# A gate group's silus queued behind a head's casts, and attention begun two filler steps sooner, in a hybrid attention and recurrence layer

## The chip, the core and the metric

The kernel runs on one core of a Trainium2 chip. TensorE (PE; PEld are its weight loads), VectorE (DVE), ScalarE (ACT) and GpSimd (POOL) each have an instruction queue of their own, and so has SyncE (SP), which here only issues transfers. The metric is the device time of one execution in microseconds, and the profile is of one execution taken by the hardware profiler.

## The reference

One layer on a residual stream x of 512 tokens by 2048 features: an RMSNorm, one input projection, an attention group beside a gated recurrence, a gate on each, and one output projection.

```python
h = rms_norm(x, norm_w)
proj = jnp.einsum('bsd,de->bse', h, w_in)                 # 2048 -> 4608
q, k, v, g_attn, xr, g_lru = jnp.split(proj, SPLITS, axis=-1)
attn_out = attention_group(q, k, v, q_norm_w, k_norm_w)   # 8 heads of 128, 2 key heads
lru_out = lru_group(xr, conv_w, conv_b, ...)              # two scans, added
mixed = jnp.concatenate([rms_norm(attn_out, attn_norm_w) * jax.nn.silu(g_attn),
                         rms_norm(lru_out, lru_norm_w) * jax.nn.silu(g_lru)], axis=-1)
return x + jnp.einsum('bse,ed->bsd', mixed, w_out)
```

In the attention group q and k get an RMSNorm and a rotary embedding per head, then softmax(q k / sqrt(128)) v over all 512 tokens. All is float32.

## The kernel before

Every operand of a matmul is split into a high and a low part of a shorter format, and `mm3` (L151) forms a product from three matmuls, high by high, high by low and low by high. A weight chunk is 256 rows by 512 columns: loaded into the ring `wr` (L205, on SP), cast by ScalarE to `wh` (L216) and subtracted by VectorE to `wl` (L217).

The stages are: the projection of the recurrence's input, with the recurrences woven into the next projections; keys and values; two query groups; then the stage that the change touches; the last gate projection; and the output projection (L901) with pre-added weights. Those pre-added weights are made by transfers between DRAM blocks, which run during the earlier stages: `last_sums` (L792) hands out one for each score step of the attention, first eight accumulating transfers on POOL (L777), then eight copies on SP (L774), then sixteen accumulating ones.

The stage in question weaves two generators on TensorE, in an order written out by hand (`manual_schedule` for PE, and for SP too):

- `gates` (L1129) is the filler: the projections of three gate groups of 512 columns, 32 filler steps each. A filler step is six matmuls into one of four PSUM banks `pj`; four steps use up one weight chunk, and eight chunks fill the four banks of a group. With the 33rd step the group's four banks are evacuated (`evac_bc`, L390, VectorE, raised to the highest priority) and `gate` (L676) emits the group's four silus at once, on the evacuated tiles `ev` in place (L682, ScalarE). Four products with the recurrence's output `hs` follow, one at every fourth filler step (L686). The first two groups do so inside this stage; the third's gate comes later, with `sig` given.
- `attention` (L649) is the chain. `turned` (L580) transposes a head's queries on TensorE (L548) and splits them: ScalarE casts the high part (L552), VectorE subtracts the low one (L553). Score step i stands for head h = i // 4 and token block t = i % 4. `weights` (L588) does its scores (three matmuls), their maximum `mx` on VectorE (L598), the exp on ScalarE (L600), the reciprocal of the sum (L601), the scaling on POOL (L602) and a 32 by 32 block transposition on VectorE into `u` (L603). At t = 0 of the next head `moved` (L608) writes `u` aside to DRAM (`pd`, L611), and at t = 2 it reads it back turned (`pt`, four transfers, L616) and splits it into `ph` by two casts on ScalarE (L624) and `pl` by two subtractions on VectorE (L625); `pt`, `ph` and `pl` have one buffer each. `values` (L629) multiplies `ph` and `pl` with the values, at score step 4h + 10 for head h: 12 matmuls. `first` in `weights` queues the maximum and exp of step 4h + 9 behind the casts and subtractions of head h.

`weave` takes BEGIN filler steps first and STEPS behind each score step; BEGIN is 12 (three chunks), STEPS 2.

TensorE and SP follow the program's order here. The order on ScalarE, VectorE and POOL is set when the kernel is built, by a planner that simulates the program with costs of its own and issues, among what is ready, what has the higher priority; `high_priority(n)` raises a block as if it stood n instructions earlier (AHEAD is 600, used for weight loads too), and `issue_after(ins)` queues what a block puts on `ins`'s engine behind `ins`. On the chip each engine keeps to that order.

Of the kernel before, what the change touches and what calls it, by code (L numbers as in the profile page):

```python
# [13 lines left out]
AF = mybir.ActivationFunctionType  # L14
# [22 lines left out]
AHEAD = 600  # L37
# [5 lines left out]
WARM, WARM2 = 14, 5  # L43


BEGIN, STEPS, LATE = 12, 2, 3


H = 256
# [13 lines left out]
def hybrid_kernel(  # L63
# [20 lines left out]
    nc = tc.nc  # L84
# [45 lines left out]
    def at(tag, bufs, shape, dt=F32):  # L130
        return pools["att"].tile([P, *shape], dt, tag=tag, bufs=bufs, name=nm(tag))
# [60 lines left out]
    def v1(r):  # L192
        return vec[:, r : r + 1]
# [350 lines left out]
    def turn(rot, h):  # L544

        pt = mm()
        for t in range(NT):
            nc.tensor.transpose(pt[:, t * P : (t + 1) * P], rot[t][:, h, :], ident)  # L548
        return pt

    def split_ps(pt, hi, lo):
        nc.scalar.copy(hi, pt)  # L552
        nc.vector.tensor_sub(lo, pt, f(hi))  # L553
# [26 lines left out]
    def turned(rot, h):  # L580

        q = at("q", 2, (2, SEQ), F32R)
        split_ps(turn(rot, h), q[:, 0, :], q[:, 1, :])
        return q[:, 0, :], q[:, 1, :]

    last_scale = [None]

    def weights(q, g, t, turned_, first=()):  # L588

        qh, ql = q  # L590
        tt = slice(t * P, (t + 1) * P)
        sc = mm()
        mm3(sc, qh[:, tt], ql[:, tt], kth[g], ktl[g], True, True)
        mx, sm = (at(n, 6, (1,)) for n in ("mx", "sm"))
        with ExitStack() as stack:
            for ins in first:
                stack.enter_context(tc.issue_after(ins))
            nc.vector.tensor_reduce(mx, sc, axis=AX.X, op=ALU.max, negate=True)  # L598
            p = at("p", 3, (SEQ,))
            nc.scalar.activation(p, sc, AF.Exp, bias=mx, accum_out=sm)  # L600
        nc.vector.reciprocal(sm, sm)  # L601
        last_scale[0] = nc.gpsimd.tensor_scalar(p, p, sm, 0.0, op0=ALU.mult, op1=ALU.add).ins  # L602
        nc.vector.transpose(  # L603
            turned_[:, :, :, t, :].rearrange("p a s c -> p s a c"),
            p.rearrange("p (s a c) -> p s a c", a=NQ, c=B),
        )

    def moved(turned_):  # L608

        aside_ = dram.tile([P, NQ, NT * P], F32, name=nm("pd"), tag="pd", bufs=NH)  # L610
        nc.sync.dma_start(aside_, turned_.rearrange("p a s t c -> p a (s t c)"))  # L611
        yield
        pt = at("pt", 1, (NQ, NT, P))
        src = aside_.rearrange("(i r) a x -> a r i x", r=B)
        for a in range(NQ):
            nc.sync.dma_start(  # L616
                pt[a * B : (a + 1) * B].rearrange("p i s x -> p i (s x)"), src[a]
            )
        hi, lo = at("ph", 1, (NT, SEQ), F32R), at("pl", 1, (NT, SEQ), F32R)
        hi4, lo4 = (v.rearrange("p s (i x) -> p i s x", i=NQ) for v in (hi, lo))  # L620
        for s in range(0, NT, 2):
            ss = slice(s, s + 2)
            last = [
                nc.scalar.copy(hi4[:, :, ss], pt[:, :, ss]).ins,  # L624
                nc.vector.tensor_sub(lo4[:, :, ss], pt[:, :, ss], f(hi4[:, :, ss])).ins,  # L625
            ]
        yield hi, lo, last

    def values(h, hi, lo):  # L629

        gs = slice(h // G * HD, (h // G + 1) * HD)
        o = mm()
        for s in range(NT):
            mm3(o, vh[s][:, gs], vl[s][:, gs], hi[:, s], lo[:, s], s == 0, s == NT - 1)
        if h % 2 == 0:
            ap_[h // 2] = aring.tile([P, 2, SEQ], F32, name=nm("av"))
        av, asum = ap_[h // 2][:, h % 2, :], sums["a"]
        nc.vector.tensor_copy(
            av.rearrange("p (t i c) -> p i t c", i=NQ, c=B),
            o.rearrange("p (i t c) -> p i t c", i=NQ, c=B),  # L640
        )
        if h == 0:
            nc.scalar.activation(asum, av, AF.Square)
        else:
            sq = at("p", 3, (SEQ,))
            nc.scalar.activation(sq, av, AF.Square)
            nc.gpsimd.tensor_add(asum, asum, sq)

    def attention(rots, transfers):  # L649

        qs, pts = {h: turned(rots[0], h) for h in range(1)}, {}
        yield BEGIN
        last = NH * NT
        for i in range(last + NT + LATE):
            h, t = divmod(i, NT)
            if i < last:
                if t == 0:
                    u = at("u", 2, (NQ, NT, NT, B))
                first = pts[h - 2][2] if h > 1 and t == 1 else ()
                weights(qs[h], h // G, t, u, first)  # L660
                next(transfers, None)
                if t == 0 and h + 1 < NH:
                    qs[h + 1] = turned(rots[(h + 1) // G], (h + 1) % G)
                if t == NT - 1:
                    pts[h] = moved(u)
            if t == 0 and 0 < h <= NH:
                next(pts[h - 1])
            if t == 2 and 0 < h <= NH:
                pts[h - 1] = next(pts[h - 1])
            h, t = divmod(i - LATE, NT)  # L670
            if t == NT - 1 and h > 0:
                values(h - 1, *pts.pop(h - 1)[:2])
            yield STEPS + (last <= i < last + NT)


    def gate(gs, pairs, row, sig):  # L676

        for e, g in enumerate(gs):
            if e == 0 or sig:
                ss = [sig()] if sig else gs  # L680
                for s, src in zip(ss, [g] if sig else gs):
                    nc.scalar.activation(s, src, AF.Silu)  # L682
            s = ss[0] if sig else g
            yield 4
            dst = pairs[e // 2][:, e % 2, :]
            nc.vector.scalar_tensor_tensor(dst, dst, v1(row + e), s, op0=ALU.mult, op1=ALU.mult)  # L686
# [409 lines left out]
    rots = []  # L1096
# [32 lines left out]
    def gates():  # L1129
        todo = iter(())  # L1130
        for n, (c0, row) in enumerate(((C_GL, R_LN), (C_GL + SEQ, R_LN + 4), (C_GA, R_AN))):
            acc, wait = [], 0
            for k, _ in enumerate(proj_feat(c0, acc, take=take)):
                if n == 0 and k >= 16 and k % 4 == 0:
                    normed(hp[k // 4 - 4])
                if wait == 0:
                    wait = next(todo, 99)
                wait -= 1
                yield
            if n < 2:  # L1140
                todo = gate(evac_bc(acc), hp[2 * n : 2 * n + 2], row, None)
            else:
                late.extend(evac_bc(acc))
# [4 lines left out]
    with tc.manual_schedule(engines={mybir.EngineType.SP}):  # L1148
        weave(fill, attention(rots, last_sums()))
# [23 lines left out]
    def later():  # L1173
        yield 2
        with tc.high_priority():
            r = group_rstd(sums["a"], "r_a", NH * HD)
        yield 4
        with tc.high_priority():
            rows(gbc, r, lambda: fin_s((P, NT, P), F32R))
        for pair in ap_[:2]:  # L1180
            normed(pair)
        yield 4
        todo = gate(late, ap_[:2], R_AN, fin_s)
        for _ in range(3):
            yield next(todo)
        build(4, ap_[0], [hring.tile([P, 7, H], F32R, name=nm(t)) for t in ("mh", "ml")])
        yield from todo
        for pair in ap_[2:]:
            normed(pair)
# [15 lines left out]
    def last_gates():  # L1205
        gs = evac_bc(acc)
        yield
        drain(gate(gs, ap_[2:], R_AN + 4, fin_s))
        yield
        yield  # L1210
        build(5, ap_[1], kept("out", 5))
        yield
        yield
        build(6, ap_[2], kept("out", 6))
        yield
        build(7, ap_[3], kept("out", 7))
        yield
# [49 lines left out]
```

## Time and profile before

| | us |
|---|---|
| time, median of 3 runs (lowest, highest) | 651.07 (650.69, 651.70) |
| the profiled execution: its time | 651.64 |
| its span, first to last instruction | 649.9 |
| TensorE busy | 636.7 |
| VectorE busy | 490.3 |
| ScalarE busy | 339.9 |
| the stage with the attention, first to last score matmul | 272.4 to about 411 |

A row of the timeline gives start and length in us, the engine, the line of the kernel, the operation, the tile written and those read, the shapes, the number of instructions in one row and, in brackets, how long the engine stood idle before it and what ended that. A row of several instructions has the time from the first's start to the last's end. A matmul's length is longer than the distance to the next one's start, since matmuls overlap: distances of starts tell the pace. A row of waits names the engine that waited, the tile and line, what it waited for, and the total, number and longest of those waits.

### The profile page before, as it was taken

How to read it: one execution, taken by the hardware profiler on the slowest of the kernel's cores; microseconds unless marked ns; L12 is line 12 of the kernel's file. 1: busy time of each engine (PE TensorE's matmuls, PEld its weight loads, DVE VectorE, ACT ScalarE, POOL GpSimd, SP SyncE). 2: the span in 40 equal slices, each digit the busy share in tenths (PEclk: the TensorE clock that was granted, in tenths of full speed). 3: DMA queues.
4: the chain of work that ended last, by engine and by line, in shares of the span. 5: the costliest groups of instructions: out<-in, count | busy, mean ns of one | idle time of the engine just before them, and what ended most of it. 6: DMA issues, size and time to landing. Idle time of an engine off the chain costs nothing.

```text
span 649.9 us, 8237 instructions
## 1 busy us (share of the span) xinstructions
PE 636.7 (98%) x2835; PEld 522.9 (80%) x2835; DVE 490.3 (75%) x788; ACT 339.9 (52%) x582; POOL 102.4 (16%) x137
## 2 busy tenths in 40 slices
PE   9999999999999999999899979999999999999996
PEld 7888888888888888888688758888888888888885
DVE  5889689977688963855877786547987867787775
ACT  3533899489856615434643464435545544434441
POOL 0000100112013301243123414301000001020010
PEclk9999999999999999999999989999999999999999
DMA  9844685857467331359889789982336676797152
GB/s 293 290 136 124 143 208 150 198 152 163 127 194 264 99 97 33 98 96 262 273 233 220 195 219 213 237 243 76 97 102 222 187 267 206 270 357 235 65 196 97
DMA packets 62074, 119.23 MB, mean 183 GB/s; under 512 B 5336, under 2 KB 15696, under 8 KB 61008
## 3 DMA queue, kind: packets, MB, share of 16 engines
q1 hardware_dynamic: 54000, 100.87, 49.1%
q0 software_dynamic: 7712, 17.31, 14.5%
q10 hardware_dynamic: 320, 0.53, 0.3%
q8 instruction: 22, 0.36, 0.2%
q14 instruction: 20, 0.16, 0.1%
HBM read 106.10 MB, written 33.55 MB: 215 GB/s over the span
## 4 chain that ended last, share of the span: by engine, by line
PE 81%; issue 6%; POOL 4%; DVE 3%; DMA 3%; ACT 2%; DVEq 0%; POOLq 0%; ACTq 0%
PE pj L152 16%; PE pj L153 16%; PE pj L154 16%; PE mm L901 11%; PE pj L901 9%; PE mm L153 3%; PE mm L154 3%; PE mm L152 3%; POOL p L602 2%; POOL t L777 1%; PE mm L242 1%; DMA wr<-in_x_dram 1%; DMA pd<-u 1%; PE pj L308 1%; DMA pt<-pd 1%
## 5 line engine op out<-in xcount | busy, mean ns | idle before, releaser
L152 PE MATMUL pj<-x,wh 128*128 128x512 f32 x376 | 148.2, 394 | 0.0
L154 PE MATMUL pj<-x,wl 128*128 128x512 f32 x376 | 146.9, 391 | 0.0
L153 PE MATMUL pj<-x,wh 128*128 128x512 f32 x376 | 146.8, 391 | 0.0
L216 ACT CAST wh<-wr 128x512 fp32r<-128x512 f32 x143 | 84.2, 618 | 88.1 <-PE pj L154 26.0
L217 DVE TENSOR_TENSOR wl<-wr,wh 128x512 fp32r<-128x512 f32 x144 | 101.7, 742 | 29.1 <-ACT wh L216 29.0
L753 ACT CAST wh<-wr 128x1024 fp32r<-128x1024 f32 (+1 forms) x72 | 60.6, 860 | 75.1 <-PE mm L901 35.3
L754 DVE TENSOR_TENSOR wl<-wr,wh 128x1024 fp32r<-128x1024 f32 (+1 forms) x72 | 68.6, 985 | 25.0 <-ACT wh L753 24.9
L154 PEld LDWEIGHTS pj<-x,wl 128*128 128x128 f32 x376 | 70.7, 188 | 15.2
L152 PEld LDWEIGHTS pj<-x,wh 128*128 128x128 f32 x376 | 70.8, 188 | 14.7
L153 PEld LDWEIGHTS pj<-x,wh 128*128 128x128 f32 x376 | 70.8, 188 | 14.6
L152 PE MATMUL pj<-wh,x 128*128 128x512 f32 x192 | 74.9, 390 | 0.0
L154 PE MATMUL pj<-wh,x 128*128 128x512 f32 x192 | 74.7, 389 | 0.0
L153 PE MATMUL pj<-wl,x 128*128 128x512 f32 x192 | 74.7, 389 | 0.0
L777 POOL DMA_DIRECT2D t<-in_w_out_dram x40 | 34.4, 867 | 101.6 <-DMA t<-in_w_out_dram 101.1
L901 PE MATMUL mm<-wh,mh 128*128 128x512 f32 x128 | 49.8, 389 | 0.0
L901 PE MATMUL mm<-wl,mh 128*128 128x512 f32 x128 | 49.8, 389 | 0.0
L901 PE MATMUL mm<-wh,ml 128*128 128x512 f32 x128 | 49.8, 389 | 0.0
L600 ACT ACTIVATE p<-mm,mx 128x512 f32<-128x512 f32 x32 | 22.0, 688 | 51.6 <-DVE mx L598 51.4
L154 PEld LDWEIGHTS pj<-wh,x 128*128 128x128 f32 x192 | 36.0, 188 | 7.6
L152 PEld LDWEIGHTS pj<-wh,x 128*128 128x128 f32 x192 | 36.1, 188 | 7.4
L153 PEld LDWEIGHTS pj<-wl,x 128*128 128x128 f32 x192 | 36.1, 188 | 7.4
L602 POOL TENSOR_SCALAR p<-p,sm 128x512 f32<-128x512 f32 x32 | 24.7, 772 | 103.6 <-DVE sm L601 97.7
(204 smaller groups left out, 1062.0 us busy)
## 6 DMA issues: line engine op xcount, KB each, us to landing
wr<-in_w_in_dram SPq DMA_DIRECT2D x71, 512.0 KB, 4.1
wr<-in_w_out_dram SPq DMA_DIRECT2D x24, 512.0 KB, 5.1
t<-in_w_out_dram POOLq DMA_DIRECT2D x40, 256.0 KB, 6.1
wr<-t SPq DMA_DIRECT2D x40, 256.0 KB, 4.7
pd<-u SPq DMA_DIRECT2D x8, 1024.0 KB, 6.6
pt<-pd SPq DMA_DIRECT2D x32, 256.0 KB, 6.1
t<-in_w_out_dram SPq DMA_DIRECT2D x24, 256.0 KB, 5.8
t<-t SPq DMA_DIRECT2D x16, 256.0 KB, 7.3
```

The costliest lines, as they stand in the source:

```text
L152: nc.tensor.matmul(acc, lh, rh, start=start, stop=False)
L153: nc.tensor.matmul(acc, lh, rl, start=False, stop=False)
L154: nc.tensor.matmul(acc, ll, rh, start=False, stop=stop)
L216: copy(hi, raw[:, k, :])
L217: nc.vector.tensor_sub(lo, raw[:, k, :], f(hi))
L242: nc.tensor.transpose(pt[:, t * P : (t + 1) * P], xc[:, t, ks], ident)
L600: nc.scalar.activation(p, sc, AF.Exp, bias=mx, accum_out=sm)
L602: last_scale[0] = nc.gpsimd.tensor_scalar(p, p, sm, 0.0, op0=ALU.mult, op1=ALU.add).ins
L753: nc.scalar.copy(hi[:, to], b)
L754: nc.vector.tensor_sub(lo[:, to], b, f(hi[:, to]))
L777: nc.gpsimd.dma_start(dst, src, accum_op=ALU.add)
L901: nc.tensor.matmul(dst[s], lh[:, ts_], rh, start=i == 0 and j == 0, stop=i == 7 and j == 2)
```

## The change

Three edits. BEGIN goes from 12 to 10 filler steps. The first head's queries are turned and split inside `high_priority(AHEAD)`. And `pts`, the table of heads whose probabilities are under way, becomes visible to `gate`, which queues its silus behind the second high-part cast of every head in it that has its parts (an entry that is a tuple; `parts[2][0]` is that cast on ScalarE).

```diff
-BEGIN, STEPS, LATE = 12, 2, 3
+BEGIN, STEPS, LATE = 10, 2, 3
...
     last_scale = [None]
+    pts = {}
...
     def attention(rots, transfers):
 
-        qs, pts = {h: turned(rots[0], h) for h in range(1)}, {}
+        with tc.high_priority(AHEAD):
+            qs = {0: turned(rots[0], 0)}
         yield BEGIN
...
         for e, g in enumerate(gs):
             if e == 0 or sig:
                 ss = [sig()] if sig else gs
-                for s, src in zip(ss, [g] if sig else gs):
-                    nc.scalar.activation(s, src, AF.Silu)
+                with ExitStack() as stack:
+                    for parts in pts.values():
+                        if isinstance(parts, tuple):
+                            stack.enter_context(tc.issue_after(parts[2][0]))
+                    for s, src in zip(ss, [g] if sig else gs):
+                        nc.scalar.activation(s, src, AF.Silu)
```

When the gates with `sig` run, after the attention, `pts` is empty and nothing is queued behind anything.

## The prediction

> **What bounds the kernel now.** The page's first row comes first: TensorE is busy in all but 2% of the span. So time can only come out of the places where it stands still or slows down, and the view of waits on TensorE names them.
>
> ```profile
> PE 636.7 (98%) x2835; PEld 522.9 (80%) x2835; DVE 490.3 (75%) x788; ACT 339.9 (52%) x582; POOL 102.4 (16%) x137
> ...
> PE mm L152 <- ACT ph L624: 3.9, 2, 3.4
> PE mm L153 <- DVE pl L625: 2.9, 3, 1.5
> ```
>
> Both large waits are for the split probabilities `ph` and `pl` of a head, in `values`. The stretches of 10 us show where (columns: start and end, length, busy PE, PEld, DVE, ACT, POOL, granted clock, DMA share, GB/s):
>
> ```profile
> 310.00:320.00 10.00, 7.78 (x33) 5.89 (x33) 9.89 (x16) 7.00 (x13) 1.36 (x2) 1.00 0.80 234
> ...
> 380.00:390.00 10.00, 5.93 (x17) 4.12 (x16) 9.21 (x13) 6.86 (x11) 0.56 (x1) 0.75 0.87 247
> 390.00:400.00 10.00, 10.00 (x41) 8.12 (x40) 5.48 (x12) 3.58 (x10) 6.61 (x7) 0.91 0.93 163
> ```
>
> In the second place the granted clock falls too, to 0.75 and 0.91 in these stretches. TensorE's timeline at both places, with an undisturbed head (346 us) between them as the measure:
>
> ```profile
> 308.77 0.40 PE L154 MATMUL mm<-kt,q 128*128 128x512 f32 x1
> 309.72 0.50 PE L152 MATMUL mm<-ph,v 128*128 128x512 f32 x1 [0.55 <-ACT ph L624]
> 311.77 0.50 PE L153 MATMUL mm<-pl,v 128*128 128x512 f32 x1 [1.55 <-DVE pl L625]
> ...
> 314.11 0.50 PE L153 MATMUL mm<-pl,v 128*128 128x512 f32 x1 [0.67 <-DVE pl L625]
> ...
> 315.38 0.39 PE L152 MATMUL pj<-x,wh 128*128 128x512 f32 x1
> ...
> 346.48 0.39 PE L154 MATMUL mm<-kt,q 128*128 128x512 f32 x1
> 349.28 0.39 PE L154 MATMUL mm<-ph,v 128*128 128x512 f32 x1
> ...
> 380.92 0.40 PE L154 MATMUL mm<-kt,q 128*128 128x512 f32 x1
> 384.69 0.56 PE L152 MATMUL mm<-ph,v 128*128 128x512 f32 x1 [3.37 <-ACT ph L624]
> 385.95 0.80 PE L153 MATMUL mm<-pl,v 128*128 128x512 f32 x1 [0.70 <-DVE pl L625]
> ...
> 391.97 0.39 PE L152 MATMUL pj<-x,wh 128*128 128x512 f32 x1
> ```
>
> From a head's last score matmul to its last value matmul are 12 starts; undisturbed they take 349.28 - 346.48 = 2.80 us, 0.233 each. The first filler matmul behind is start 13, so 3.03 us. At the first place it comes 315.38 - 308.77 = 6.61 us later: **3.58 us lost**. At the second, 391.97 is start 16 (three filler matmuls, 0.23 each, are in between), due after 3.72 us, but comes after 11.05: **7.33 us lost**, 4.07 of it the marked waits and most of the rest 14 starts at 0.43 us (385.95 to 391.97) instead of 0.23. Together 10.9 us.
>
> Why `ph` is late is on ScalarE:
>
> ```profile
> 305.77 1.28 ACT L682 ACT_TABLE_LOAD   x1
> 307.06 0.63 ACT L682 ACTIVATE ev<-ev 128x512 f32<-128x512 f32 x1
> ...
> 308.63 1.98 ACT L624 CAST ph<-pt 128x1024 fp32r<-128x1024 f32 x2
> ...
> 311.56 1.15 ACT L682 ACTIVATE ev<-ev 128x512 f32<-128x512 f32 x2
> 314.73 1.28 ACT L600 ACT_TABLE_LOAD   x1 [2.03 <-DVE mx L598]
> ...
> 377.71 1.28 ACT L682 ACT_TABLE_LOAD   x1
> ...
> 381.81 0.63 ACT L682 ACTIVATE ev<-ev 128x512 f32<-128x512 f32 x1 [1.55 <-DVE ev L390]
> ...
> 383.61 1.98 ACT L624 CAST ph<-pt 128x1024 fp32r<-128x1024 f32 x2
> ```
>
> A gate group's silus (L682) and their table load stand ahead of the `ph` casts: two silus at 307, four from 379 on, where ScalarE also waits for an evacuation (L390). That the data was not what was late, the chain of waits says:
>
> ```profile
> 294.61 4.99 DMA pt<-pd
> ```
>
> The transposed probabilities of head 0 had landed by 299.6, 9 us before their casts began.
>
> **The change, part by part.** I count score steps i (four to a head, `weights`) and filler steps (six matmuls, 12 x 6 starts from 255.95 to 272.41 below, 1.372 us each).
>
> *Silus behind the high parts.* The gate group is emitted with filler step 33. Before, that followed score step 10 = 12 + 2 x 10; now it follows 11, and likewise 27 in place of 26. `pts` then holds head 1 (or 5) as a tuple, so the silus queue behind that head's second `ph` cast. There is one `ph` buffer, so this cast in turn comes after head 0's values: all silus leave the place ahead of `ph` 0 and `ph` 4. Nothing is added: the same 8 silus, the same table loads. Removed from the path: up to 3.58 + 7.33 us.
>
> What then sets `ph` is the planner's usual order, `ph` behind the exp of step 4h+8. Heads 3 and 5 show its margin:
>
> ```profile
> 362.96 2.32 DVE L625 TENSOR_TENSOR pl<-pt,ph 128x1024 fp32r<-128x1024 f32 x2
> 364.20 0.19 PEld L153 LDWEIGHTS mm<-pl,v 128*128 128x128 f32 x1 [0.46 <-DVE pl L625]
> ...
> 401.62 2.31 DVE L625 TENSOR_TENSOR pl<-pt,ph 128x1024 fp32r<-128x1024 f32 x2
> 405.08 0.40 PE L152 MATMUL mm<-ph,v 128*128 128x512 f32 x1
> ```
>
> Head 5's first `pl` half ends about 402.8, and the second value matmul wants it at 405.3: 2.5 us to spare. Head 3 had -0.46, by the weight load's wait. The gate heads carry in addition the evacuations L390 on VectorE, which are raised above everything:
>
> ```profile
> 309.89 0.69 DVE L390 TENSOR_TENSOR ev<-pj,rbc 128x512 f32<-128x512 f32 x1
> ```
>
> With the values now before filler steps 31 and 32, two of the four banks can be evacuated ahead of them: 2 x 0.69 = 1.4 us in front of `pl`. By head 5's margin that costs 0, by head 3's 0.46 + 1.4 = 1.9 us. I take 0.4 a gate, nearer to head 5, since the gate products (L686), which need the silus, leave this place on VectorE with them: **0.8 us left of the 10.9**, bounds 0 and 3.8.
>
> *Where the silus go.* Behind head 1's casts ScalarE has a gap now:
>
> ```profile
> 324.28 1.99 ACT L624 CAST ph<-pt 128x1024 fp32r<-128x1024 f32 x2
> ...
> 330.25 0.69 ACT L600 ACTIVATE p<-mm,mx 128x512 f32<-128x512 f32 x1 [2.94 <-DVE mx L598]
> ```
>
> The block is 1.28 + 2 x 1.15 + 1.28 = 4.9 us; 2.9 hide in the gap, so the exps of steps 13 and 14 come some 2 us late. The next thing this could hold is head 2's `ph` behind exp 16, with head 5's 2.5 us margin: I cost it at nothing. Without the gap it would be 4.9 - 2.5 = 2.4 us a gate. Queued behind the silus are the four gate products (L686), now some 12 us later; their result is read only after the attention.
>
> On the price of the switch the Trainium skill speaks against the change: "ScalarE: Activation LUTs", section "What ACT_TABLE_LOAD costs", puts about 1.38 us of drain on top of the 1.28 us load. Here the load at 305.77 ends at 307.05 and the silu starts at 307.06, so no row shows the drain; with it the block would be 7.6 us by an estimate from that page, and about 2.2 us a gate would be lost.
>
> *First scores two filler steps sooner* (BEGIN 10). All attention work moves 2.74 us ahead of the projection: scores, exps, `pd` and `pt` transfers on SP, one accumulating DMA (L777) on POOL per step. On SP the `pd` and `pt` issues stay ahead of the same weight loads; a 256 KB `t<-t` copy moves in front of some, which ring and fetch-ahead cover. By itself this gains nothing: TensorE runs the same matmuls. What it needs is query 0:
>
> ```profile
> 255.95 0.48 PE L152 MATMUL pj<-x,wh 128*128 128x512 f32 x1
> ...
> 268.40 0.59 ACT L552 CAST q<-mm 128x512 fp32r<-128x512 f32 x1 [0.84 <-DVE ev L536]
> ...
> 269.02 1.29 DVE L217 TENSOR_TENSOR wl<-wr,wh 128x512 fp32r<-128x512 f32 x2
> 270.22 0.68 DVE L553 TENSOR_TENSOR q<-mm,q 128x512 fp32r<-128x512 f32 x1
> ...
> 272.41 0.40 PE L152 MATMUL mm<-kt,q 128*128 128x512 f32 x1
> ```
>
> The scores move to 255.95 + 10 x 1.372 = 269.67; the third matmul of `mm3`, 0.47 us later at 270.14, wants the low part, which now ends at 270.90. *Queries at higher priority*: the cast at 268.40 waits for a rope product on VectorE, so it can't go much sooner; but the subtraction can pass the two L217 and end near 269.7. So the wait is 0 (it passes) to 0.76 us (it doesn't); I take **0.2**. If ScalarE stands at this cast, two weight casts stand behind it, with one chunk (four filler steps) of cover; without it 1.1 us.
>
> *Sum.* The profiled execution is 651.64 us (span 649.9 and 1.74 around it). 651.64 - 10.9 + 0.8 + 0.2 = 641.7. It lies 0.57 above the median of 651.07, so **641.2 us** against the median; own range 639.8 (all 10.9 and head 3's 0.46 saved) to 644.8 (all bounds: 3.0 and 0.56 more).
>
> The clock term rests on rows: 4.07 us of waits brought 0.75 and 0.91, while 2.77 us at the first place left 1.00. The Trainium skill, "TensorE: Matmul & The Clock Gate", Part 1, gives the array a half-rate clock after an idle window of about 3.4 us and one busy window to recover. The trace agrees with the 0.43 us starts; by it, too, a remaining wait of 1 to 2 us costs no clock.
>
> **The rivals.** *The silu block is cut up.* If the planner sets exps between the silus, they need another pair of table loads, 2.56 us: exps 1.9 + 2.6 = 4.5 us late, less the 2.5 us margin 2.0 us on heads 2 and 6, together 4.0: **645.2**. For it: the evacuations come in one by one, and silus with them (two, a pause, two, above). Against: behind `ph` 1 all four evacuations are done.
>
> *A switch holds ScalarE for longer than its load.* If each of the block's two switches took a second load's length, 1.28 us, the block would be 7.4 us, the exps again 4.5 late: **645.2**. Against it the silu starts 0.01 us behind its load. This is the drain of the page named above.
>
> *The gain is given back elsewhere:* the `ph` casts stay late for another reason on the two engines, so that only the silus' place changes: **651**. Against it is the landing at 299.6.
>
> *Slower.* The half-chunk shift puts weight splits in front of `pl`. Filler chunks now end before odd score steps, in the middle of each head's cast and split:
>
> ```profile
> 351.93 4.12 DVE L217 TENSOR_TENSOR wl<-wr,wh 128x512 fp32r<-128x512 f32 x2
> ...
> 353.00 1.89 POOL L647 TENSOR_TENSOR asum<-asum,p 128x512 f32<-128x512 f32 x1
> ```
>
> A pair took 4.12 us here instead of 1.29, beside POOL work. If such a pair lands before `pl` in every head, 4.12 - 2.5 = 1.6 us is lost eight times, 13 us, on top of the 641.2: **654**. It decides from 9.9 / 8 = 1.24 us a head on, where nothing of the gain is left. Against: the chunk's buffers come free only at score step 4h+9, when the casts behind exp 4h+8 have usually begun, and the other pair of each head moves away from the values' POOL work.
>
> **How the numbers follow.** Forecast (641.2) 0.66; cut-up silus 0.10 and longer switches 0.04 (645.2); given back (651) 0.05; slower (654) 0.15. About 0.2%, here 1.3 us, is what a measurement of this kernel can tell from no change: faster is below 649.8, 0.66 + 0.10 + 0.04 = 0.80; same 0.05; slower 0.15. The range leaves out the last two cases and starts with the forecast's own: 639.8 to 649.8.
>
> **What would show it.** Right: L682 only behind the `ph` casts of heads 1 and 5; the waits for `ph` and `pl` on TensorE down from 6.8 us to under 2; granted clock 1.00 from 300 to 400; first score matmul near 269.7. Wrong: new TensorE waits at heads 2 and 6 (cut-up silus, or longer switches), in every head's `values` with L217 ahead of L625 (slower), or at the first score for `q`.

## The result and the profile after

| | before | after |
|---|---|---|
| time, median (lowest, highest), us, 20 runs each on the same chip | 651.57 (649.77, 652.95) | 650.84 (647.40, 653.39) |
| span of the profiled execution, us | 649.9 | 649.9 |
| ratio to before, 95% interval | | 0.9991 [0.9978, 1.0005] |

No change that this measurement can tell, where 641.2 us were forecast. (New lines of the kernel stand up to six later: the exp is L601, `pd` L612, `pt` L617, `ph` L625, `pl` L626, the silus L688, the accumulating transfers L783.) The waits of TensorE in the changed kernel:

```profile
PE pj L152 <- ACT wh L216: 3.3, 1, 3.3
PE mm L153 <- DVE pl L626: 3.0, 3, 1.7
...
PE pj L154 <- DVE wl L217: 0.8, 1, 0.8
PE mm L154 <- DVE q L553: 0.6, 1, 0.6
```

The waits for `ph` are gone, those for `pl` are as large as before, and the largest is new: a weight chunk. The stretches show where:

```profile
310.00:320.00 10.00, 9.54 (x44) 7.86 (x45) 8.05 (x16) 4.85 (x11) 2.06 (x3) 1.00 0.91 262
...
380.00:390.00 10.00, 10.00 (x45) 8.13 (x44) 8.05 (x15) 3.22 (x7) 4.60 (x5) 1.00 1.06 236
...
420.00:430.00 10.00, 6.85 (x31) 5.26 (x29) 2.68 (x4) 3.60 (x6) 0.00 (x0) 1.00 0.95 256
430.00:440.00 10.00, 9.11 (x32) 7.02 (x33) 4.67 (x7) 2.24 (x5) 0.00 (x0) 0.83 0.33 110
```

The stretch from 380 us is full, at full clock (5.93 us and 0.75 before). From 420 to 440 us, behind the last score (this stretch is called the tail below), 4 us are missing and the clock falls to 0.83, where the kernel before lost nothing. TensorE's timeline at heads 0 and 4, and in the tail:

```profile
306.71 0.39 PE L154 MATMUL mm<-kt,q 128*128 128x512 f32 x1
310.46 0.50 PE L153 MATMUL mm<-pl,v 128*128 128x512 f32 x1 [1.74 <-DVE pl L626]
311.74 0.39 PE L152 MATMUL pj<-x,wh 128*128 128x512 f32 x1
...
378.76 0.50 PE L153 MATMUL mm<-pl,v 128*128 128x512 f32 x1 [0.98 <-DVE pl L626]
...
426.46 0.39 PE L154 MATMUL pj<-x,wl 128*128 128x512 f32 x1
430.10 0.50 PE L152 MATMUL pj<-x,wh 128*128 128x512 f32 x1 [3.25 <-ACT wh L216]
431.63 0.80 PE L154 MATMUL pj<-x,wl 128*128 128x512 f32 x1 [0.79 <-DVE wl L217]
...
434.79 0.48 PE L152 MATMUL pj<-x,wh 128*128 128x512 f32 x1
435.10 0.39 PE L153 MATMUL pj<-x,wh 128*128 128x512 f32 x1
```

Head 0 takes 311.74 - 306.71 = 5.03 us where 3.03 are due: 2.0 lost, in place of 3.58. From 426.46 to 435.10 are 11 starts, due in 2.5 us at 0.227 each: 6.1 us lost, 3.4 of them the wait of the first and the rest a second wait of 0.79 and starts 0.43 apart. Summing every distance of two starts above 0.28 us, less 0.232, between 254 and 640 us gives TensorE's standing time in the one profiled execution of each kernel, which the experiments below are compared by (small rows left out, so that rows need not add up):

| us | first score | head 0 | head 4 | heads 5 to 7 and tail, 395 to 440 | sum |
|---|---|---|---|---|---|
| before | 0 | 3.59 | 7.33 | 0 | 12.7 |
| after | 0.99 | 2.01 | 1.25 | 6.59 | 13.1 |

So 7.7 us were gained at the two heads, as the change means to, and 7.6 us given back at the first score and behind the last head. What makes the chunk late is read backwards from its cast, over ScalarE and SP, each of which keeps its order:

```profile
393.08 0.43 SPq L205 DMA_DIRECT2D wr<-in_w_in_dram  x1
...
401.32 0.40 PE L154 MATMUL mm<-kt,q 128*128 128x512 f32 x1
...
403.55 1.14 ACT L216 CAST wh<-wr 128x512 fp32r<-128x512 f32 x2 [3.10 <-DMA wr<-in_w_in_dram]
...
411.94 0.34 SPq L612 DMA_DIRECT2D pd<-u  x1
...
418.88 2.26 SPq L617 DMA_DIRECT2D pt<-pd  x4
421.17 1.89 SPq L205 DMA_DIRECT2D wr<-in_w_in_dram  x3
427.54 1.99 ACT L625 CAST ph<-pt 128x1024 fp32r<-128x1024 f32 x2 [6.25 <-DMA pt<-pd]
429.44 2.17 ACT L216 CAST wh<-wr 128x512 fp32r<-128x512 f32 x4
```

The load issued at 393.08 is cast only at 403.55, after ScalarE stood idle 3.10 us waiting for it, with the last head's exps queued behind. So the last `pd` comes at 411.94, 10.6 us behind the last score matmul (401.32). The four `pt` transfers are held until `pd` has landed, and the next chunk's load (421.17) stands behind them on SP; its cast, at 429.44, stands behind the last head's `ph` casts, which wait 6.25 us for `pt`. The same places before:

```profile
400.12 0.43 SPq L205 DMA_DIRECT2D wr<-in_w_in_dram  x1
...
410.53 1.14 ACT L216 CAST wh<-wr 128x512 fp32r<-128x512 f32 x2 [3.24 <-DMA wr<-in_w_in_dram]
...
411.12 0.40 PE L154 MATMUL mm<-kt,q 128*128 128x512 f32 x1
...
416.31 0.34 SPq L611 DMA_DIRECT2D pd<-u  x1
```

This load was just as slow before (10.4 us to its cast), but TensorE reached the last score at 411.12, 9.8 us later, and `pd` followed 5.2 us behind it. TensorE came 9.8 us sooner, `pd` only 4.4. The lost time at the gates had hidden a late load.

### The profile page after: what moved, and what is told of

Its sections match the earlier page's. It is cut to its first block, busy times and chain, and to the rows that moved or that the text cites. A ratio compares the mean times of both kernels' runs of the same rounds, so it can differ in the third digit from the quotient of the medians.

```text
span 649.9 us, 8252 instructions
## 1 busy us (share of the span) xinstructions
PE 635.1 (98%) x2835; PEld 521.3 (80%) x2835; DVE 486.9 (75%) x788; ACT 340.3 (52%) x582; POOL 102.9 (16%) x137
## 4 chain that ended last, share of the span: by engine, by line
PE 71%; DMA 11%; issue 7%; POOL 5%; DVE 3%; ACT 2%; SPq 1%; ACTq 0%; DVEq 0%; POOLq 0%
PE pj L154 14%; PE pj L152 14%; PE pj L153 14%; PE mm L907 11%; PE pj L907 9%; DMA wr<-in_w_in_dram 5%; DMA pd<-u 3%; POOL p L603 2%; PE mm L153 2%; PE mm L154 2%; PE mm L152 2%; POOL t L783 1%; DMA wr<-in_x_dram 1%; DMA pt<-pd 1%; PE mm L242 1%
## 5 line engine op out<-in xcount | busy, mean ns | idle before, releaser
L217 DVE TENSOR_TENSOR wl<-wr,wh 128x512 fp32r<-128x512 f32 x144 | 99.5, 725 | 29.1 <-ACT wh L216 28.8
L760 DVE TENSOR_TENSOR wl<-wr,wh 128x1024 fp32r<-128x1024 f32 (+1 forms) x72 | 68.6, 983 | 25.0 <-ACT wh L759 24.8
L783 POOL DMA_DIRECT2D t<-in_w_out_dram x40 | 34.7, 876 | 102.2 <-DMA t<-in_w_out_dram 101.1
L601 ACT ACTIVATE p<-mm,mx 128x512 f32<-128x512 f32 x32 | 21.9, 688 | 49.7 <-DVE mx L599 44.0
```

What stands on the lines that cost most here:

```text
L217: nc.vector.tensor_sub(lo, raw[:, k, :], f(hi))
L760: nc.vector.tensor_sub(lo[:, to], b, f(hi[:, to]))
L783: nc.gpsimd.dma_start(dst, src, accum_op=ALU.add)
```

## The experiments

Ratios are to the kernel before on the same chip, with 95% intervals. In the diffs a minus is the changed kernel where nothing else is said.

**Each half of the change alone, and the place of the late load.** My theory was that the early begin made the tail's stall, by putting one load behind `pt` on SP.

e1, the silus' queueing alone:

```diff
-BEGIN, STEPS, LATE = 10, 2, 3
+BEGIN, STEPS, LATE = 12, 2, 3
...
-        with tc.high_priority(AHEAD):
-            qs = {0: turned(rots[0], 0)}
+        qs = {0: turned(rots[0], 0)}
```

> Only the silus' place is changed; the first scores stay 12 filler steps behind the query. Theory (the early begin costs what the silus gain): the stall at 426 to 435 us, 6.1 us in the changed kernel, is absent, because the loads of two weight chunks stand ahead of the last head's four transposing transfers on SP as before; the first score waits for nothing (0.99 us in the changed kernel); of the 10.9 us at heads 0 and 4 some 1 to 3.3 are left. So 12.7 - 10.9 + 1 to 3.3 us of standstill, a time 7.6 to 9.9 us under that of the kernel before: a ratio of 0.985 to 0.988. Rival (moving the silus frees no time by itself, the gain is given back wherever the attention is shifted to): 0.996 to 1.002, with a new stall of 5 us or more at some other place.

e2, the early begin alone:

```diff
-                with ExitStack() as stack:
-                    for parts in pts.values():
-                        if isinstance(parts, tuple):
-                            stack.enter_context(tc.issue_after(parts[2][0]))
-                    for s, src in zip(ss, [g] if sig else gs):
-                        nc.scalar.activation(s, src, AF.Silu)
+                for s, src in zip(ss, [g] if sig else gs):
+                    nc.scalar.activation(s, src, AF.Silu)
```

> Only the first scores begin two filler steps sooner; the silus stay where the planner puts them. Theory: the stall of 6.1 us behind 426 us and the 1.0 us at the first score are there without the silus' queueing, so both come from the early begin alone. At heads 0 and 4 the high parts now come ahead of some silus by the planner's own order, so part of the 10.9 us may go without the queueing too. If it does not go: 12.7 + 7.1 us of standstill, ratio 1.010 to 1.012. If it goes as in the changed kernel (3.3 left): ratio 0.998 to 1.002, and the queueing is worth nothing beside the early begin. Rival (the tail's stall comes from the silus' queueing): no stall of more than 1 us between 420 and 440 us.

e3, one filler step moved ahead in the tail:

```diff
-            yield STEPS + (last <= i < last + NT)
+            yield STEPS + {last: 1, last + 1: 2, last + 2: 1}.get(i, 0)
```

> The changed kernel with the four extra filler steps behind the last scores given out as 1, 2, 1, 0 in place of 1, 1, 1, 1: the next chunk's load is then emitted ahead of the last head's transposing transfers on SP, and its splits ahead of that head's casts. Theory (the tail stalls because that chunk's load stands behind a transfer that waits): the 6.1 us behind 426 us fall to under 1, nothing else moves, ratio 0.989 to 0.992 to the kernel before. Rival (the stall is the last head's own chain, from its scores over its transfers to its values, or another bound of the projection there): 4 us or more of standstill between 415 and 445 us remain, ratio 0.996 to 1.001.

e4, that step's load alone (`early` fetches a chunk that `take` then doesn't fetch):

```diff
+            if i == last + 1:
+                early()
```

> The changed kernel with that one chunk's load alone issued one step sooner, ahead of the last head's transposing transfers on SP; its splits stay behind that head's casts on ScalarE. Theory, if the load is what is late: the stall of 6.1 us behind 426 us falls to under 1 us, as with the moved step. Theory, if the place of the splits on ScalarE is what is late: a wait of about 2 us for the casts of the chunk behind the last head's two casts (2.0 us each) remains, with the slow starts behind it, 2 to 5 us. Rival (neither): 6 us remain. Ratios 0.990, 0.993 to 0.997, and 0.999.

| us | first score | head 0 | head 4 | 395 to 440 | sum | median | ratio |
|---|---|---|---|---|---|---|---|
| e1 silus | 0 | 2.49 | 1.60 | 7.40 | 12.6 | 652.13 | 1.002 [1.0003, 1.0036] |
| e2 begin | 0.99 | 1.42 | 3.68 | 3.32 | 10.6 | 649.91 | 0.999 [0.9971, 1.0008] |
| e3 step | 1.00 | 1.42 | 1.25 | 7.71 | 13.4 | 650.81 | 0.999 [0.9969, 1.0011] |
| e4 load | 1.03 | 1.42 | 1.25 | 7.75 | 12.6 | 651.93 | 1.0001 [0.9986, 1.0016] |

My theory fell. Without the early begin the silus' queueing frees 6.8 us at heads 0 and 4 (10.92 - 4.09) and loses 7.4 behind them. The timeline of e1 there:

```profile
395.86 0.44 SPq L205 DMA_DIRECT2D wr<-in_w_in_dram  x1
...
406.69 1.14 ACT L216 CAST wh<-wr 128x512 fp32r<-128x512 f32 x2 [4.88 <-PE pj L153]
...
415.34 0.79 PE L152 MATMUL pj<-x,wh 128*128 128x512 f32 x1 [1.97 <-ACT wh L216]
...
419.30 0.80 PE L154 MATMUL pj<-x,wl 128*128 128x512 f32 x1 [2.74 <-DVE wl L217]
```

The same load again takes until 406.69, 10.8 us behind its issue, with ScalarE idle for 4.88. (The bracket names the matmul that frees the buffer; but the load is what came last: by its record in the trace it took 10.8 us to land, until 406.6.) In e3 and e4 the moved load took part of the stall away, but it put another in its place: the fourth `pt` transfer of the last head (in e4 the last two) now stands on SP behind a later load, which in e3 is issued only at 427.59. The timeline of e3:

```profile
427.59 0.39 SPq L205 DMA_DIRECT2D wr<-in_w_in_dram  x1
428.02 0.47 SPq L617 DMA_DIRECT2D pt<-pd  x1
```

The last head's values then waited for `ph`, and 5.0 us were lost from 431 us on (5.9 in e4). So e3 and e4 do not tell the order on SP from the rest. e2 had a smaller tail loss than I expected, 1.69 us: TensorE came there later, having lost more at heads 4 and 5 (3.68 and 1.63 us). It also shows that the early begin alone frees 5.8 us at heads 0 and 4 (10.92 - 5.10), so the two halves of the change reach for much the same stalls. What all six kernels share is that the sum stays between 10.6 and 13.4 us: time gained early is lost at the last heads, as if something else set their pace. The DMA engines are the candidate; their share over the 140 us from 290 to 430 us was 0.93 before and 0.93 after. Much of this is not needed so soon: the accumulating transfers on POOL that hand the output projection its pre-added weights.

**The accumulating transfers moved.** e5 to e8 take the last 16 (t1 and t4) or 8 (t4) of the 24 out of the attention and issue them with the last gate projection. The diff is that of 16; with 8, the first 24 of all 32 transfers stay, and one follows every fourth filler step:

```diff
-        weave(fill, attention(rots, last_sums()))
+        transfers = last_sums()
+        weave(fill, attention(rots, itertools.islice(transfers, 16)))
...
-    fill = proj_feat(C_GA + SEQ, acc, take=take)
+    def with_late(fill):
+        for k, _ in enumerate(fill):
+            if k % 2 == 0:
+                next(transfers, None)
+            yield
+
+    fill = with_late(proj_feat(C_GA + SEQ, acc, take=take))
```

> The silus' queueing alone, and 16 of the 24 accumulating copies on POOL (the sums t1 and t4, one behind each of the last 16 score steps) issued behind the attention instead, one per two filler steps of the last projection. The same copies, another place. New theory (the sixteen DMA engines bound the stretch from 290 to 430 us: their share there is 0.93 before, 0.93 after and 0.92 with the silus alone, so whatever TensorE saves earlier it waits for later, in a late weight chunk): by the software queue's 14.5% of the span, 94 us for 17.31 MB, the sixteen copies of 256 KB are 23 us by their bytes; the share falls to about 0.8, the stall at 413 to 422 us (7.0 us) goes, and the time is 7 to 9 us under before, ratio 0.986 to 0.990. Rival (the stall at 413 us is an order of ScalarE's or VectorE's queue that has nothing to do with how full the DMA engines are): stall of 5 us or more stays between 405 and 435 us, ratio 0.998 to 1.003.

> The changed kernel with the same 16 copies issued behind the attention. DMA theory: the 6.1 us behind 426 us shrink to under 3 (what the fixed place of the load on SP keeps), the 1.0 us at the first score and some 3.3 us at heads 0 and 4 stay: ratio 0.989 to 0.995. Theory of the fixed order alone: the 6.1 us stay in full, ratio 0.998 to 1.000.

> The kernel before with the same 16 copies issued behind the attention, the silus where they were. DMA theory as I hold it: the stalls at heads 0 and 4 there (10.9 us) come from ScalarE's order, not from the transfers, and stay; no stall behind 405 us was there to go; ratio 0.997 to 1.001. If instead the moved copies by themselves are what helps (rival), 0.986 to 0.990 as with the silus. So the gain of the silus' queueing would be the difference of this run and the run with both.

> As the first, but only the 8 copies of t4, those of the last 8 score steps, are moved behind the attention. By the DMA theory, in proportion: some 11 us of transfers less, beginning near 385 us, ahead of the late chunk of 406 us; most of the stall at 413 to 422 us goes, ratio 0.988 to 0.993. If the copies matter only over the whole stretch, 0.993 to 0.997. Rival of a fixed order: 0.998 to 1.003.

| us | head 0 | head 4 | 395 to 440 | behind 445 | sum | median | ratio |
|---|---|---|---|---|---|---|---|
| e5 silus, 16 moved | 2.26 | 1.25 | 5.89 | 7.27 | 17.3 | 657.43 | 1.0089 [1.0074, 1.0104] |
| e6 after, 16 moved | 1.42 | 1.24 | 7.43 | 0.54 | 12.3 | 652.24 | 1.0012 [1.0004, 1.0021] |
| e7 before, 16 moved | 4.05 | 2.97 | 4.23 | 7.38 | 19.3 | 659.24 | 1.0117 [1.0094, 1.0139] |
| e8 silus, 8 moved | 2.19 | 1.59 | 5.72 | 0.54 | 11.1 | 649.75 | 0.9975 [0.9964, 0.9986] |

None met its expectation, since POOL has nothing else to do there: it issued the moved transfers at once, from 410 us on, into the tail. With 16 of them, e5 and e7 also lost 4.8 us at 448 to 450 us, where TensorE waits for a sum that POOL has behind them. But e8 shows the mechanism at work both ways. The load of 393.84 there takes 5.8 us in place of 10.8 and only 1.24 us are lost near 413; then come the transfers, and the DMA view from 405 to 430 us gives the loads:

```profile
wr<-in_w_in_dram SPq DMA_DIRECT2D x5, 512.0 KB, 12.1
```

12.1 us in the median, and 4.48 us are lost from 422 us on.

**The transfers held until the tail is over.** e9 to e12, against the runs above: POOL first copies one column of the attention's scale, which is there near 450 us, so that the transfers wait for it (they are handed out at every second filler step, the 16 of e10 at every one):

```diff
             r = group_rstd(sums["a"], "r_a", NH * HD)
+        held = const([P, 1], "held")
+        last_scale[0] = nc.gpsimd.tensor_copy(held, r[:, :1]).ins
...
-            if k % 2 == 0:
+            if k > 3 and k % 2 == 0:
```

> The silus' queueing alone, and the 8 copies of t4 behind the attention, held on POOL until the scale of the attention's norm is there (near 450 us), so that they run neither in the attention nor in its tail. Theory (weight chunks are late because their transfers share the sixteen DMA engines with these copies): in the run with the 8 copies merely moved, the load that had taken 10.8 us took 5.8 and the 5.6 us at 413 us fell to 1.2; but the copies then ran from 410 us on, the two loads of 411.7 took 12.2 and 15.0 us, and 4.5 us were lost behind 421 us. Held, those loads take 8 us or less, the 4.5 us go as well, some 5.5 to 6.5 us of standstill are left of 12.7: ratio 0.988 to 0.992. Rival (the order on SP, the load behind the last head's first transfer, makes that stall whatever runs beside it): 4 us or more stay at 420 to 430 us, ratio 0.996 to 0.999.

> The same with all 16 copies of t1 and t4 held until near 450 us. Theory: no more is gained in the attention than with 8, since with 8 nothing but heads 0 and 4 is left there: ratio 0.988 to 0.992, if the sums t1 are there in time for the first output chunks; a wait for them near 490 us would show in the loads of t1 and cost up to 5 us, 0.996. Rival as above: 0.996 to 0.999.

> The changed kernel with the 8 copies of t4 held the same way. Its tail load stands behind the last head's transposing transfers on SP, which wait for the transfer before them to land. If only the length of the transfers is at fault: that wait shrinks by 2 us and the load by 2 to 3 us, and of the 6.1 us behind 426 us under 2.5 are left: ratio 0.990 to 0.994. If the order on SP and ScalarE makes it: 4 us or more stay, 0.996 to 1.000.

> The kernel before with the 8 copies of t4 held the same way. Theory: its 10.9 us at heads 0 and 4 are ScalarE's order and stay, nothing else is there to gain, ratio 0.998 to 1.002; the silus' queueing then is worth its gain only where the transfers leave room. Rival (the held copies themselves are the gain): 0.988 to 0.994.

| us | first score | head 0 | head 4 | 395 to 440 | sum | median | ratio |
|---|---|---|---|---|---|---|---|
| e9 silus, 8 held | 0 | 2.75 | 1.73 | 1.26 | 6.9 | 649.48 | 0.9966 [0.9953, 0.9980] |
| e10 silus, 16 held | 0 | 2.59 | 1.26 | 1.25 | 5.9 | 648.71 | 0.9958 [0.9945, 0.9971] |
| e11 after, 8 held | 0.94 | 1.43 | 1.26 | 0 | 4.7 | 647.65 | 0.9940 [0.9926, 0.9953] |
| e12 before, 8 held | 0 | 5.01 | 6.97 | 0 | 13.1 | 655.44 | 1.0057 [1.0042, 1.0072] |

The standing times are what the theory asked for: the tail's stall is gone, in the changed kernel altogether, though its load keeps its place on SP; 16 held gain no more there than 8; and the kernel before keeps its own stalls. The times are not (only e11 lies in its expected range, at its upper end): all are some 4 us longer than their standing times say. Something slows every matmul a little. The stretch from 500 to 600 us, in which TensorE never waits, in e11:

```profile
500.00:600.00 100.00, 100.00 (x435) 81.28 (x434) 75.47 (x94) 43.46 (x54) 8.86 (x14) 1.00 0.74 247
```

and in e13, below, which differs in that one tile (the instructions of the two traces stand in the same order on every engine):

```profile
500.00:600.00 100.00, 100.00 (x442) 82.68 (x442) 76.17 (x94) 43.87 (x56) 8.89 (x14) 1.00 0.74 246
```

435 matmuls against 442 in the same time, at the same granted clock; the mean distance of two starts from 500 to 640 us is 0.2308 and 0.2268 us.

**Without the new tile; traffic and queue apart.** e13 (changed kernel), e14 (before) and e18 (silus alone) hold the 8 transfers with a copy into a constant that is there already; against e11:

```diff
-        held = const([P, 1], "held")
-        last_scale[0] = nc.gpsimd.tensor_copy(held, r[:, :1]).ins
+        last_scale[0] = nc.gpsimd.tensor_copy(table, r[:, :1]).ins
```

> The changed kernel with the 8 copies of t4 held until the attention's scale is there, without the extra constant tile: the copy that holds them writes into a constant that is there already. Theory (the tile shifts the tiles behind it and with them the pace of the matmuls): 0.227 us apart behind 500 us, 4.7 us of standstill, 651.5 - 12.7 + 4.7 = 643.5 us, ratio 0.986 to 0.990. Rival (the held copies themselves slow the matmuls): 0.231 us apart, 647.6 us as before, ratio 0.994.

> The kernel before with the 8 copies held in the same way, without the extra tile. Theory: its 10.9 us at heads 0 and 4 stay and the copies were in nobody's way there, so ratio 0.998 to 1.002; the difference to the run above is the worth of the change where the transfers leave room, 7 to 8 us. Rival (the copies cost): ratio 1.005, as with the tile.

e15 puts plain copies of the same size at the last eight score steps of e13, issued by SP:

```diff
+    t5 = dram.tile([NP, P, SEQ + 16], F32, name="t5", tag="t5")[:, :, :SEQ]
+
+    def plain():
+        for m in range(NP):
+            copy_to((t5[m], block(m, 1, 1)))
+            yield
...
-        weave(fill, attention(rots, itertools.islice(transfers, 24)))
+        weave(fill, attention(rots, itertools.chain(itertools.islice(transfers, 24), plain())))
```

> As e13, and at each of the last 8 score steps a plain copy of 256 KB from DRAM to DRAM, issued by SP, into a tensor that nobody reads: traffic put back without POOL. If the traffic on the sixteen DMA engines makes the chunk late: the stall behind 425 us comes back, 3 us or more, and the time is 3 to 7 us over that of e13. If POOL's time or its queue was it: no stall there, within 1 us of e13.

And e17, against e15:

```diff
-            copy_to((t5[m], block(m, 1, 1)))
+            with tc.issue_after(last_scale[0]):
+                nc.gpsimd.dma_start(t5[m], block(m, 1, 1))
```

> As e13 (the copies of t4 held), and at each of the last 8 score steps a plain copy of 256 KB from DRAM to DRAM, issued by POOL in the place of the accumulating one, into a tensor that nobody reads. If POOL's queue (its issue time, its own share of the DMA engines) makes the chunk late: the load behind the sixth head's transfer takes 9 us or more, the stall behind 425 us is back with 3 us or more, 647 to 651 us, ratio 0.993 to 0.999. If it is the accumulating (each copy reads twice what it writes): that load stays near 6 us, no stall, 643.5 to 645.5 us, ratio 0.987 to 0.990.

> The silus' queueing alone (first scores 12 filler steps behind the query), the copies of t4 held, no extra tile. From the runs with the tile (655.44, 649.48 and 647.65 us for none, the silus, and both) the silus are worth some 6.0 of the 7.8 us: with 651.05 us for none and 644.37 for both, about 645.5 to 646 us, ratio 0.989 to 0.992. If the early begin made half of it or more: 647.5 us or above, 0.993.

| us | first score | head 0 | head 4 | 395 to 440 | sum | median | ratio |
|---|---|---|---|---|---|---|---|
| e13 after, held | 1.00 | 1.42 | 1.25 | 0 | 4.7 | 644.37 | 0.9886 [0.9871, 0.9901] |
| e14 before, held | 0 | 4.13 | 6.25 | 0 | 11.4 | 651.05 | 0.9988 [0.9974, 1.0002] |
| e18 silus, held | 0 | 2.20 | 1.60 | 1.24 | 6.9 | 645.68 | 0.9915 [0.9901, 0.9929] |
| e15 plain from SP | 1.00 | 1.43 | 1.25 | 0 | 5.1 | 643.60 | 0.9876 [0.9862, 0.9889] |
| e17 plain from POOL | 0.98 | 1.43 | 1.25 | 1.48 | 6.7 | 645.38 | 0.9913 [0.9898, 0.9929] |

Holding the transfers is worth nothing that can be told to the kernel before (0.9988), as expected; to the changed one it is worth some 6.5 us (650.84 to 644.37; ratios 0.9991 and 0.9886, whose intervals lie far apart). So the change is worth 651.05 - 644.37 = 6.7 us where the transfers leave room (7 to 8 were expected), and the standing time falls by as much, from 11.4 to 4.7. Of the 6.7 some 5 are the silus: 5.4 by the times (to 645.68), but e18 ran on another chip, and by the ratios, each to the kernel before on its own chip, it is 4.8. The remaining 1.3 to 1.9 us are what the early begin adds to the silus; the early begin alone with the transfers held was not run. The timeline of e13, for the rows shown of after:

```profile
392.41 0.43 SPq L205 DMA_DIRECT2D wr<-in_w_in_dram  x1
...
400.66 1.31 ACT L216 CAST wh<-wr 128x512 fp32r<-128x512 f32 x2 [0.89 <-ACT p L601]
...
401.81 0.40 PE L154 MATMUL mm<-kt,q 128*128 128x512 f32 x1
...
408.87 0.34 SPq L612 DMA_DIRECT2D pd<-u  x1
...
413.84 1.74 SPq L617 DMA_DIRECT2D pt<-pd  x4
415.62 4.65 SPq L205 DMA_DIRECT2D wr<-in_w_in_dram  x3
```

ScalarE no longer waits for the load; `pd` is 7.1 us behind the last score in place of 10.6, `pt` follows after 5.0 in place of 6.9, and the tail's load is issued at 415.62 in place of 421.17, 5.6 us sooner (6.0 counted from the last score): about the 6.1 us that the tail had lost. The order on SP, which I blamed first, is the same.

How the loads fare beside each kind of copy is in the DMA view from 380 to 410 us (queue, packets, MB, share of the sixteen engines; then the issues with their size and median time to landing). After:

```profile
q1 hardware_dynamic: 2370, 5.22, 64.7%
q0 software_dynamic: 802, 1.48, 33.7%
...
wr<-in_w_in_dram SPq DMA_DIRECT2D x3, 512.0 KB, 9.3
```

e17, plain copies from POOL:

```profile
q0 software_dynamic: 575, 1.90, 24.8%
...
wr<-in_w_in_dram SPq DMA_DIRECT2D x4, 512.0 KB, 7.6
```

e13, none:

```profile
wr<-in_w_in_dram SPq DMA_DIRECT2D x4, 512.0 KB, 5.9
```

A load takes 5.9 us beside no copies, 7.6 beside plain ones from POOL, 9.3 beside accumulating ones; beside the plain ones of SP it takes 6.1, and no stall came back (e15). The expectation of e17 had 9 us or more for the queue and near 6 for the accumulating, and the 7.6 lies between. So POOL's queue explains a part (1.5 us of stall in e17), and the accumulating seems to be the larger one (6.1 us in the tail of the changed kernel); each rests on one trace, and the bytes moved are not equal. e15 is not quite the same traffic either: SP issues its copies ahead, POOL between the score steps.

**What is left at heads 0 and 4.** e16, as e13 with the low parts raised on VectorE:

```diff
-                nc.vector.tensor_sub(lo4[:, :, ss], pt[:, :, ss], f(hi4[:, :, ss])).ins,
...
+            with tc.high_priority():
+                last.append(
+                    nc.vector.tensor_sub(lo4[:, :, ss], pt[:, :, ss], f(hi4[:, :, ss])).ins
+                )
```

> As e13, with the subtractions that make the low parts raised to the priority of the evacuations on VectorE. If VectorE's order makes what is left at heads 0 and 4 (1.43 and 1.26 us): both go down to 0.3 or less, 2 us under e13, ratio 0.983 to 0.987. If the low parts are late because the high parts are (the casts wait for the last of four transposing transfers): 1 us or more stays at head 0, and the time is that of e13.

642.45 us, 0.9857 [0.9844, 0.9871], the fastest, though its interval overlaps that of e15. At head 0 nothing is lost any more (1.42 in e13); at head 4 2.52 us are, twice as much as in e13. The standing time as a whole is 4.6 us, as in e13 (4.7), so it does not explain the 1.9 us between the two times; what does is open. The timeline of e16 at head 4:

```profile
375.58 1.25 DVE L390 TENSOR_TENSOR ev<-pj,rbc 128x512 f32<-128x512 f32 x2
376.76 2.34 DVE L627 TENSOR_TENSOR pl<-pt,ph 128x1024 fp32r<-128x1024 f32 x2
378.02 0.50 PE L153 MATMUL mm<-pl,v 128*128 128x512 f32 x1 [2.25 <-DVE pl L627]
```

Two evacuations still stand ahead of `pl` there. So VectorE's order makes the rest at head 0; at head 4 this edit did not undo it.

## Why the prediction was wrong

**The step that failed** is the one that costed the transfers at nothing, in "First scores two filler steps sooner": "On SP the `pd` and `pt` issues stay ahead of the same weight loads; ... which ring and fetch-ahead cover. By itself this gains nothing". The cover was measured by the kernel that was slow. There TensorE came late to the last heads, and the load of 400.12 could take 10.4 us for nothing. With the stalls gone, the same load is the bound of the last heads: 6.6 us of standstill between 410 and 440 us in the changed kernel, 7.4 in e1 without any shift of the scores. Moved out of the way in e13 and e14, the transfers let the same change gain 6.7 us. So the error is not in the shift alone; the whole sum subtracted 10.9 us as though the next limit were further away than that, and it stood right behind. The rows were there: DMA share 0.93 in a stretch that the prediction quotes for its clock, and a cast that waits 3.24 us for its load.

**The term "up to 10.9 us removed, 0.8 left"** was right in kind and mis-sized: 3.26 us are left at heads 0 and 4 (2.01 and 1.25), and 2.67 where the transfers are held (e13). With the term below it gives what the change is worth there, 4.13 + 6.25 (e14) - 2.67 - 1.00 = 6.7 us, and not the 9.9 of the forecast. At head 4 it is the two evacuations of 0.69 each ahead of `pl`, as written, without head 5's margin, which I had leaned on; at head 0 two weight splits come in front of the second `pl` half besides, in the timeline of after:

```profile
307.98 1.29 DVE L217 TENSOR_TENSOR wl<-wr,wh 128x512 fp32r<-128x512 f32 x2 [0.48 <-ACT wh L216]
...
309.19 1.22 DVE L626 TENSOR_TENSOR pl<-pt,ph 128x1024 fp32r<-128x1024 f32 x1
```

Both lie inside the bounds given (0 to 3.8). The wait for `pl` is 3.0 us, where under 2 was to show.

**The term "first scores 0.2"** came at the bad end (0.76): the first score is at 269.51, as forecast (269.67), but 0.99 us of standing time arises there, since the subtraction did not pass the splits:

```profile
268.85 1.28 DVE L217 TENSOR_TENSOR wl<-wr,wh 128x512 fp32r<-128x512 f32 x2
...
270.05 0.68 DVE L553 TENSOR_TENSOR q<-mm,q 128x512 fp32r<-128x512 f32 x1
```

Raising the first queries does nothing: built without that edit, the changed kernel has the same instructions in the same order on all five engines, so it was not run. Weight loads are raised by the same 600.

**Right:** the silus stand only behind the `ph` casts of heads 1 and 5 (first table load at 322.42, behind casts from 320.41), with one switch there and one back for each group; no drain shows (322.42 + 1.28 = 323.70, the first silu starts at 323.71); TensorE does not wait at head 2, and at head 6 only for 0.24 us (0.50 us of standing time from 412.5 us on); the clock is 1.00 from 300 to 400 us.

**The clock** bears the prediction out only in part. In the tail of the changed kernel the starts are 0.43 us apart behind a wait of 3.25 us. The Trainium skill, "TensorE: Matmul & The Clock Gate", Part 1, has the half rate follow an idle window of about 3.4 us; this wait comes near it. But that 1 to 2 us of waits cost no clock, as the prediction concluded, does not hold in every execution: in e14 two waits of 0.63 and 1.54 us at head 0 are followed by starts 0.43 us apart, where 2.77 us of waits in the kernel before left the clock at 1.00. The rows of e14:

```profile
312.27 0.79 PE L153 MATMUL mm<-pl,v 128*128 128x512 f32 x1 [1.54 <-DVE pl L625]
...
310.00:320.00 10.00, 8.23 (x28) 6.39 (x29) 9.35 (x15) 7.50 (x14) 1.58 (x1) 0.83 0.83 247
```

What decides it was not tried.

**Misread, without a price:** "landed by 299.6" was the first of head 0's four `pt` transfers. In the changed kernel the casts of 304.22 still wait 1.29 us for the last of them.

**The rivals:** "given back" has the right time, with a wrong mechanism (`ph` late for another reason); the gain was given back 35 to 115 us later, by loads. Splits ahead of `pl` in every head did not come: head 3 loses 0.32 us, as before.

## What to carry to other kernels

A stall that you remove may have been the slack of the next limit: before subtracting it, look how late the transfers behind it already are (casts that wait for a DMA, share of the DMA engines near 1) and ask what happens when they are wanted that much sooner. When a gain vanishes, compare the same event in both traces against TensorE's place (here the last score to the last `pd`, 5.2 against 10.6 us), and not the sums of waits. Work for later stages that shares the DMA engines with such a stretch is moved past it, and held there by something real, since an idle queue issues it at once.

## What was not expected of the hardware

Accumulating transfers between DRAM blocks weigh more than their bytes: from 380 to 410 us the software queue kept the sixteen engines busy for 33.7% of 30 us with 1.48 MB, 6.8 us of all sixteen engines a MB; plain copies from the same queue (e17) took 24.8% for 1.90 MB, 3.9 us a MB, and the hardware queue beside the accumulating ones 3.7. The Trainium skill, "DMA: Bandwidth & Descriptors", section "Issuing engines are not separate DMA queues", says that transfers of all issuing engines interleave on the same sixteen DMA engines; the rise of a load from 5.9 us (e13) to 9.3 us (changed kernel) agrees.

A constant tile of 128 x 1 that one instruction writes slowed the matmuls behind 500 us from 0.2268 to 0.2308 us each: 647.65 against 644.37 us, and 655.44 against 651.05. It presumably moves the tiles behind it; which address matters was not tried.
